# Rings of blocks for scores and probabilities, and an output bank in quarters

## The chip, the core and the metric

The kernel runs on one core of a Trainium2 chip. The metric is the device time of one execution in microseconds, as the median of several runs. A core has five engines that run side by side and are ordered by semaphores: TensorE (PE) for matmuls, VectorE (DVE), ScalarE (ACT), GpSimd (POOL), and SyncE (SP), which issues DMA transfers here.

## The reference, cut to what matters

One layer of an encoder for 2048 prompt rows and 64 sample rows of width 1024. A modulated norm is followed by one input projection; its columns feed four heads of differential attention (two softmaxes, subtracted) and eight heads of forgetting attention (a softmax with a cumulative bias); each result is gated and all go through one output projection.

```python
gate, qa, ka, va, za, qb, kb, vb, zb, logf = project(xp, c_prompt, pos_p, *lw)

def diff_attention(q, k, v, mask, lam):
    s = jnp.einsum('bqhjd,bkhjd->bhjqk', q, k).astype(F32) * (A_QK_DIM ** -0.5)
    p = jax.nn.softmax(jnp.where(mask, s, -jnp.inf), axis=-1)
    a = p[:, :, 0] - lam * p[:, :, 1]
    return jnp.einsum('bhqk,bkhe->bqhe', a.astype(v.dtype), v)

def forgetting_attention(q, k, v, mask, bias):
    s = jnp.einsum('bqhd,bkhd->bhqk', q, k).astype(F32) * (B_DIM ** -0.5) + bias
    p = jax.nn.softmax(jnp.where(mask, s, -jnp.inf), axis=-1)
    return jnp.einsum('bhqk,bkhd->bqhd', p.astype(v.dtype), v)

def merge(x, gate, oa, za, ob, zb, subln_g, lam_init, w_out):
    b, t = x.shape[:2]
    oa = rms_norm(oa, subln_g) * (1.0 - lam_init)
    ga = oa.reshape(b, t, A_WIDTH) * jax.nn.silu(za)
    gb = ob.reshape(b, t, B_WIDTH) * jax.nn.silu(zb)
    o = jnp.concatenate([ga, gb], axis=-1) @ w_out
    return x + gate[:, None, :] * o
```

## The kernel before

The work is cut into eight units. Units 0 to 3 are one differential head each, units 4 to 7 two forgetting heads each; they run in the order 0, 1, 4, 5, 6, 7, 2, 3, the first two interleaved, and the output projection follows. A unit walks over eight blocks of 256 query rows and one block of the sample. A block is projected (matmuls into q with weights wc and activations hT), its queries and keys are normed on ACT, DVE and POOL (u, rs), transposed on PE (tr) and split into a high and a low half in 16 bits.

A row of attention is 128 queries, i from 0 to 15, with i+1 key blocks of 128. Each row has two streams s, which are the two softmaxes of a differential head or the two heads of a forgetting unit. A row goes through these steps:

- PE writes scores into S (`qk_pair`), DVE moves them out into E with mask, bias and maximum (`qk_chunk`).
- ACT takes the exponent in place and sums it (`row_exp`). In a forgetting unit ACT then makes the high half of the probabilities in PB (`row_hi_B`) and DVE the low half (`row_lo_B`).
- SP transposes PB into PT by DMA (`row_trans`), in pieces of eight blocks.
- PE multiplies PT with the values into the bank po (`pv`): per block a matmul of 128 columns and one of 64 in a forgetting unit.
- `outB` reads the forgetting row out of po into og: ACT copies the 64-column halves that hold a lower part, scaled by a number of the unit, DVE adds the upper ones, and two more DVE instructions multiply by the reciprocal of the sum (st) and by the gate g. `outA_sq` and `outA` do it for a differential row. og goes to DRAM (ogd), whence the output projection takes it.

E has three buffers of 16 blocks, PB two of 16, PT seven of eight. A forgetting row of fewer than eight blocks puts both streams into one buffer, a longer one takes a buffer for each. The output bank po is one bank of 512 columns, given out in halves of 256 (`O_tile`); a row takes one half.

The order is made by a planner (class `Plan`). Every step is recorded as an event with a position (`ev`), in the order of positions. The planner gives each instruction a priority from its position, from a table `SHIFT` (one number for each kind of step, engine and slot of the order) and from the buffers that it would have to free, and then lists the instructions of all engines against its own costs; they are issued in the listed order. Each engine runs its instructions strictly in that order. All instructions are issued from one line of the planner, so that the profile gives them all line L547, and tiles tell them apart.

## Time and profile before

| | before |
|---|---|
| median of 3 runs | 1586.65 us (1586.03 to 1587.31) |
| the profiled execution | 1581.7 us |
| its span | 1579.9 us |
| PE busy | 1424.7 us, 90% |
| DVE busy | 1262.2 us, 80% |
| ACT busy | 932.5 us, 59% |
| POOL busy | 508.0 us, 32% |
| DMA queue 1, share of 16 engines | 85.2% |

An engine's busy time tells how much of the span its instructions fill. An engine that waits is told by the views of waits and by the idle time in the groups of instructions, each with the event that ended the wait: "PE po <- DMA PT<-PB" is PE idle before a matmul into po until the transfer from PB to PT had landed. The rows that matter stand in their own section below.

### The profile page before, as it was taken

The numbers are of one execution on the slowest core, as the hardware profiler recorded it, in microseconds if no ns is written. First come the engines' busy times: TensorE is split into PE (matmuls) and PEld (weight loads), VectorE is DVE, ScalarE is ACT, GpSimd is POOL, SyncE is SP. The second block draws the span as 40 slices with busy tenths as digits, with TensorE's granted clock in tenths as the row PEclk, the third lists the DMA queues.
The fourth block names the chain that finished last, engine by engine and source line by source line (L and its number), as shares of the span: only waits on it lengthen the run. The fifth ranks groups of instructions, "written<-read, shape, count | busy, mean of one in ns | idle before, by whom it ended". The sixth has DMA issues, their size and how long they took to land. (4 is left out here: it accounts for less than half of the span.)

```text
span 1579.9 us, 29641 instructions
## 1 busy us (share of the span) xinstructions
PE 1424.7 (90%) x10901; PEld 726.5 (46%) x10901; DVE 1262.2 (80%) x2624; ACT 932.5 (59%) x1772; POOL 508.0 (32%) x620
## 2 busy tenths in 40 slices
PE   6799989889999998988999899988898999699998
PEld 3344445444454444444444454444444444345443
DVE  3989999889778887987798779887798789796531
ACT  2557776666567666765686667656665576453100
POOL 0268564334221112211121112113445354422322
PEclk8899999989999999999999999999999999899999
DMA  9759799659887999999999999899758656698962
GB/s 321 202 149 236 168 205 236 141 114 209 177 186 165 197 236 178 227 196 200 181 255 200 193 205 240 189 204 201 175 138 161 141 139 148 127 199 202 250 178 62
DMA packets 623133, 297.38 MB, mean 188 GB/s; under 512 B 508718, under 2 KB 596414, under 8 KB 615563
## 3 DMA queue, kind: packets, MB, share of 16 engines
q1 hardware_dynamic: 622988, 295.50, 85.2%
q8 instruction: 85, 1.39, 0.4%
q14 instruction: 60, 0.49, 0.1%
HBM read 129.05 MB, written 43.16 MB: 109 GB/s over the span
## 5 line engine op out<-in xcount | busy, mean ns | idle before, releaser
L547 PE MATMUL q<-wc,hT 128*128 128x512 f16 x3072 | 740.4, 385 | 12.3 <-DVE wc L547 2.3
L547 PEld LDWEIGHTS <-hT 128*128 128x128 f16 x3328 | 295.1, 99 | 325.2 <-issue 39.8
L547 ACT ACTIVATE E<-E,st 128x512 f32<-128x512 f32 (+15 forms) x256 | 305.9, 1196 | 155.1 <-DVE st L547 82.9
L547 PE MATMUL po<-VT,PT 128*128 128x128 f16 x3808 | 241.8, 214 | 71.8 <-DMA PT<-PB 44.3
L547 PEld LDWEIGHTS <-PT 128*128 128x128 f16 x3808 | 209.7, 99 | 144.8 <-DMA PT<-PB 61.4
L547 PE MATMUL S<-KT,qT 64*128 64x512 f16 (+3 forms) x1920 | 223.8, 352 | 24.2 <-DVE E L547 13.8
L547 DVE SCALAR_TENSOR_TENSOR PB<-E,PB 128x128 f16<-128x128 f32 (+15 forms) x128 | 165.5, 1302 | 42.4 <-ACT PB L547 42.0
L547 POOL TENSOR_SCALAR rs<-rs 128x8 f32<-128x8 f32 (+1 forms) x72 | 22.4, 311 | 525.4 <-DVE rs L547 518.0
L547 PE MATMUL y<-wc,ogT 128*128 128x512 f16 (+1 forms) x800 | 175.9, 380 | 1.1 <-DVE yt L547 0.9
L547 ACT ACTIVATE PB<-E 128x128 f16<-128x128 f32 (+15 forms) x128 | 139.2, 1103 | 47.4 <-DMA PT<-PB 46.6
L547 DVE CUSTOM_DVE_ANT_0 E<-S,nk,cf 128x1024 f32<-128x1024 f32 (+7 forms) x128 | 131.2, 1044 | 27.8 <-PE S L547 27.2
L547 PEld LDWEIGHTS <-qT 64*128 64x128 f16 x1920 | 85.5, 95 | 147.2 <-issue 83.2
L547 DVE TENSOR_SCALAR_CACHE_REDUCE E<-S,cf 128x1024 f32<-128x1024 f32 (+7 forms) x128 | 130.6, 1044 | 10.1 <-PE S L547 9.5
L547 POOL TENSOR_TENSOR u<-u,gain 128x512 f32<-128x512 f32 (+1 forms) x72 | 100.1, 1391 | 116.5 <-DVE u L547 20.2
L547 POOL TENSOR_TENSOR rs<-rs,mhalf 128x8 f32<-128x8 f32 (+1 forms) x72 | 120.7, 1676 | 5.6
L547 PEld LDWEIGHTS <-ogT 128*128 128x128 f16 (+1 forms) x800 | 76.2, 98 | 93.8 <-issue 7.4
L547 ACT ACTIVATE PB<-E,st 128x128 f16<-128x128 f32 (+7 forms) x64 | 76.7, 1199 | 56.5 <-DVE E L547 20.0
L547 ACT ACTIVATE u<-q,us 128x384 f32<-128x384 f32 x128 | 73.1, 571 | 54.9 <-PE q L547 29.4
L547 DVE SCALAR_TENSOR_TENSOR PB<-E,st,PB 128x128 f16<-128x128 f32 (+7 forms) x64 | 88.5, 1382 | 9.9 <-ACT PB L547 9.5
L547 POOL TENSOR_TENSOR yt<-yt,xr 128x512 f32<-128x512 f32 (+1 forms) x34 | 51.4, 1514 | 120.3 <-DVE yt L547 84.6
L547 POOL TENSOR_SCALAR oar<-oar 128x1 f32<-128x1 f32 (+1 forms) x68 | 31.8, 467 | 152.5 <-ACT og L547 149.4
L547 ACT ACTIVATE og<-po,us 128x128 f32<-128x128 f32 x128 | 45.9, 360 | 50.6 <-PE po L547 46.2
(222 smaller groups left out, 1764.2 us busy)
## 6 DMA issues: line engine op xcount, KB each, us to landing
hT<-hTd SPq DMA_DIRECT2D x53, 1024.0 KB, 5.8
out_dram<-u SPq DMA_DIRECT2D x128, 128.0 KB, 3.1
wc<-in_w_in_dram SPq DMA_DIRECT2D x32, 256.0 KB, 6.6
x<-in_x_prompt_dram SPq DMA_DIRECT2D x16, 512.0 KB, 4.7
hTd<-hT SPq DMA_DIRECT2D x16, 512.0 KB, 3.1
ogd<-og SPq DMA_DIRECT2D x64, 128.0 KB, 2.9
nk<-nck_d SPq DMA_DIRECT2D x16, 512.0 KB, 6.7
xr<-in_x_prompt_dram SPq DMA_DIRECT2D x16, 512.0 KB, 4.6
```

Of the source, the lines that this page charges most:

```text
L547: fn(*a, **kw)
```

## The change

- E, PB and PT become rings of 48, 32 and 56 blocks with the bytes of before (`ring_take`). A row's stream takes i+1 blocks; where they don't fit before the end, the ring starts again at its first block. The weights of the modulation, the first x, its split and the scratch of the first statistics take their space from the rings or from other buffers, and the weights are all loaded in halves.
- The bank po is given out in quarters of 128 columns. A forgetting row takes one for each stream, and `outB` runs for each stream: ACT copies 128x64 scaled by the stream's own reciprocal, DVE adds 128x64 in the same scale. `row_recip` therefore also multiplies the two reciprocals by the unit's number, on ACT. The gate is one product of 128x128 on POOL (`outB_gate`).
- `ev` takes a second position `at`. Events are recorded in the order of `at`, while the priority still comes from the first position; a row's steps now stand together in the record.
- The table `SHIFT` has other numbers throughout; the planner's other numbers are the same.
- The warming matmuls at the head are 176 of 128 columns, not 88 of 256.

```diff
-        po[0] = 256 - po[0]
-        return po[1][:, po[0]:po[0] + 256]
+        po[0] = (po[0] + 128) % 512
+        return po[1][:, po[0]:po[0] + 128]
...
+    rings = dict(E=[0, 48, st([128, 48 * 128], F32, "Ering")], PB=[0, 32, st([128, 32, 2, 128], F16, "PBring")],
+                 PT=[0, 56, st([128, 112, 128], F16, "PTring")])
+
+    def ring_take(name, n):
+        r = rings[name]
+        if r[0] + n > r[1]:
+            r[0] = 0
+        b, r[0] = r[0], r[0] + n
+        if name == "E":
+            return r[2][:, b * 128:(b + n) * 128]
+        return r[2][:, b:b + n] if name == "PB" else r[2][:, 2 * b:2 * (b + n)]
...
-        for _ in range(2 * n):
-            pe.matmul(mod_ps["w"], ident_b, ident_b.unsqueeze(1).broadcast_to([128, 2, 128]), start=True, stop=True)
+        for _ in range(4 * n):
+            pe.matmul(mod_ps["w"], ident_b, ident_b, start=True, stop=True)
...
-            if s == 0 or i >= 8:
-                E_t[g, i, s] = st([128, 2048], F32, f"E{g}_{i}_{s}", tag="E", bufs=3)
-            else:
-                E_t[g, i, 1] = E_t[g, i, 0][:, 1024:2048]
+            E_t[g, i, s] = ring_take("E", i + 1)
...
-        if s == 0 or i >= 8:
-            PB_t[g, i, s] = st([128, 16, 2, 128], F16, f"PB{g}_{i}_{s}", tag="PB", bufs=2)
-            if i < 8:
-                PB_t[g, i, 1] = PB_t[g, i, 0][:, 8:16]
+        PB_t[g, i, s] = ring_take("PB", i + 1)
...
             dve.reciprocal(out=sm[:, 6:8], in_=sm[:, 4:6])
+            act.activation(out=sm[:, 6:8], in_=sm[:, 6:8], func=AF.Copy, scale=usc[g][:, 5:6])
...
-            PT_t[g, i, s, b0 // 8] = st([128, 16, 128], F16, f"PT{g}_{i}_{s}_{b0}", tag="PT", bufs=7)
+            PT_t[g, i, s, b0 // 8] = ring_take("PT", b1 - b0)
...
-        if part == 0 and s == 0:
-            o_ps[g, i] = O_tile()
-        o = o_ps[g, i]
+        if part == 0:
+            o_ps[g, i, s] = O_tile()
+        o = o_ps[g, i, s]
...
-    def outB(g, i, j, t):
-        if t == 0:
+    def outB(g, i, j, t, s):
+
+        if t == 0 and s == 0:
             og_new(g, j)
-        o = o_ps.pop((g, i))[:, 0:256].rearrange("p (s h d) -> p s h d", s=2, h=2)
+        o, sc = o_ps.pop((g, i, s)), st_t.pop((g, i, s))[:, 6 + s:7 + s]
+        w = og_t[g, j][:, t, 64 * s:64 * s + 64]
+        act.activation(out=w, in_=o[:, 64:128], func=AF.Copy, scale=sc)
+        dve.scalar_tensor_tensor(out=w, in0=o[:, 0:64], scalar=sc, in1=w, op0=ALU.mult, op1=ALU.add)
+
+    def outB_gate(g, j, t):
         w = og_t[g, j][:, t, :]
-        w2 = w.rearrange("p (s d) -> p s d", s=2)
-        c = usc[g][:, 5:6]
-        act.activation(out=w2, in_=o[:, :, 1, :], func=AF.Copy, scale=c)
-        dve.scalar_tensor_tensor(out=w2, in0=o[:, :, 0, :], scalar=c, in1=w2, op0=ALU.mult, op1=ALU.add)
-        for s in range(2):
-            d = slice(64 * s, 64 * s + 64)
-            dve.scalar_tensor_tensor(out=w[:, d], in0=w[:, d], scalar=st_t.pop((g, i, s))[:, 6 + s:7 + s], in1=g1_t[g, j][:, t, d],
-                                     op0=ALU.mult, op1=ALU.mult)
+        pool.tensor_tensor(out=w, in0=w, in1=g1_t[g, j][:, t, :], op=ALU.mult)
         if t == 1:
             out_done(g, j)
...
-    def ev(pos, fn, *a):
-        events.append((pos, len(events), fn, a))
+    def ev(pos, fn, *a, at=None):
+
+        events.append((pos if at is None else at, len(events), fn, a, pos))
...
-                    ev(a0 + wd * 0.80, row_exp, g, i, s)
+                    b0 = a + t * 0.5 + 0.40 + 0.01 * s
+                    ev(a0 + wd * 0.80, row_exp, g, i, s, at=b0)
...
-                        ev(a + 1.52 + 0.5 * t, outB, g, i, j, t)
+                                ev(a + 1.00 + 0.5 * t + 0.25 * s + 0.23 * p / npc, pv, g, i, s, p, npc, at=b0 + 0.01 * s)
+                            ev(a + 1.27 + 0.25 * s + 0.5 * t, outB, g, i, j, t, s, at=b0 + 0.005 + 0.01 * s)
+                        ev(a + 1.54 + 0.5 * t, outB_gate, g, j, t, at=b0 + 0.02)
```

On DVE, in unit 5, where rows 11 and 12 follow each other (E_12 and S_12 belong to row 12, the last digit of S_12_0_1 is the chunk of eight blocks; ISA is the evacuation of scores), before:

```order
L547 ISA E_12_0_1246,st_12_0_1247<-S_12_0_0_1244,nk_0_0_1032,cf_196 128x1024 [waits PE_49]
L547 ISA st_12_0_1247 128x1
L547 SCALAR_TENSOR_TENSOR PB_11_0_1239<-E_11_0_1227,PB_11_0_1239 128x12x128 [waits DMAHW1_49,DMAHW0_49,Activation_49]
L547 SCALAR_TENSOR_TENSOR PB_11_1_1240<-E_11_1_1234,PB_11_1_1240 128x12x128 [waits DMAHW3_49,DMAHW2_49,Activation_49]
L547 SCALAR_TENSOR_TENSOR u_8_1241<-q_8_0_1226,us_850,lowr_1242 64x128 [waits Activation_49]
L547 TENSOR_TENSOR qT_7_1249<-tr_7_1248,qT_7_1249 128x256 [waits PE_49,Activation_49]
L547 SCALAR_TENSOR_TENSOR KT_1_1155<-tr_7_1248,sg_192,KT_1_1155 128x256
L547 SCALAR_TENSOR_TENSOR u_8_1241<-q_8_0_1226,us_850,lowr_1242 64x384
L547 ISA E_12_1_1252,st_12_0_1247<-S_12_1_0_1245,nk_1_0_1033,cf_196 128x1024 [waits DVE_49]
L547 ISA st_12_0_1247 128x1
```

and now, where the two low halves of row 11 are the rows that write PBring:

```order
L548 ISA Ering,st_12_0_947<-S_12_0_0_945,nk_0_0_806,cf_195 128x1024 [waits DVE_49,PE_49]
L548 ISA st_12_0_947 128x1
L548 ISA Ering,st_12_0_947<-S_12_1_0_946,nk_1_0_807,cf_195 128x1024 [waits DVE_49,PE_49]
L548 ISA st_12_0_947 128x1
L548 RECIPROCAL st_11_0_937<-st_11_0_937 128x2 [waits Activation_49]
L548 SCALAR_TENSOR_TENSOR og_4_913<-po,st_9_0_917,og_4_913 128x64 [waits Activation_49]
L548 SCALAR_TENSOR_TENSOR g_5_7_923<-g_5_7_923,q_7_1_926 128x128
L548 TENSOR_REDUCE rs_7_939<-sq_7_938 128x8 [waits Activation_49]
L548 SCALAR_TENSOR_TENSOR VT_1_885<-u_7_922,us_696,VT_1_885 128x2x64 [waits Activation_49] x2
L548 ISA Ering,st_12_0_947<-S_12_0_1_950,nk_0_1_877,st_12_0_947,cf_195 128x640 [waits DVE_49,PE_49]
L548 ISA st_12_0_947 128x1
L548 SCALAR_TENSOR_TENSOR PBring<-Ering,PBring 128x12x128 [waits DMAHW6_49,DMAHW7_49,DMAHW5_49,Activation_49]
```

Both streams' first chunks of row 12 stood on either side of the low halves of row 11; they now stand ahead of them, and so does the second chunk of one stream.

On DVE, in the same unit, where row 10 is read out of the bank po into og_5, before (rows that belong to other steps stand between):

```order
L547 SCALAR_TENSOR_TENSOR og_5_1265<-po,us_850,og_5_1265 128x128
L547 TENSOR_REDUCE rs_8_1267<-sq_8_1266 64x4 [waits Activation_49]
L547 SCALAR_TENSOR_TENSOR og_5_1265<-og_5_1265,st_10_0_1211,g_5_5_1148 128x64 [waits DVE_49]
L547 SCALAR_TENSOR_TENSOR og_5_1265<-og_5_1265,st_10_0_1211,g_5_5_1148 128x64
L547 SCALAR_TENSOR_TENSOR g_5_s<-g_5_s,u_8_1241 64x128
```

and now:

```order
L548 ISA Ering,st_12_0_947<-S_12_1_1_951,nk_1_1_878,st_12_0_947,cf_195 128x640 [waits DVE_49,PE_49]
L548 ISA st_12_0_947 128x1
L548 SCALAR_TENSOR_TENSOR og_5_933<-po,st_10_0_927,og_5_933 128x64 [waits Activation_49]
L548 SCALAR_TENSOR_TENSOR og_5_933<-po,st_10_0_927,og_5_933 128x64
L548 SCALAR_TENSOR_TENSOR PBring<-Ering,PBring 128x12x128 [waits DMAHW0_49]
```

Three instructions for the row, one of them over both streams, became two of 64 columns, one for each stream; the product with the gate g stands on POOL.

On PE, in unit 6, where the product of row 14 passes from its first stream to the second, before (PT_14_1_0 is the second stream's first piece):

```order
L547 MATMUL q_2_1_1609<-wc_128,hT_2_1560 128x512
L547 LDWEIGHTS PT_14_1_0_1578 [waits DMAHW3_49]
L547 MATMUL po<-VT_0_1306,PT_14_1_0_1578 128x128
L547 LDWEIGHTS PT_14_1_0_1578
L547 MATMUL po<-VT_0_1306,PT_14_1_0_1578 128x64
```

and now:

```order
L548 MATMUL tr_1_1180<-ident,u_1_1155 128x128 [waits DVE_49,Pool_49]
L548 MATMUL tr_1_1180<-ident,u_1_1155 128x128 x3
L548 LDWEIGHTS PTring [waits DMAHW0_49]
L548 MATMUL po<-VT_0_982,PTring 128x128 [waits Activation_49]
L548 LDWEIGHTS PTring
L548 MATMUL po<-VT_0_982,PTring 128x64
L548 LDWEIGHTS PTring
L548 MATMUL po<-VT_0_982,PTring 128x128 [waits DVE_49]
```

The second stream began behind a projection and waited only for its transpose; it now begins behind the transposes of tr_1 and has a wait for ACT and, two matmuls on, one for DVE, which read po.

## Rows read from the trace of the kernel before

**Rows 1.** Busy us (share of the span) and instructions of each engine, the page.
```profile
PE 1424.7 (90%) x10901; PEld 726.5 (46%) x10901; DVE 1262.2 (80%) x2624; ACT 932.5 (59%) x1772; POOL 508.0 (32%) x620
```

**Rows 2.** PE waits: us in total, times, longest us.
```profile
PE po L547 <- DMA PT<-PB: 44.3, 35, 4.4
PE tr L547 <- POOL u L547: 17.3, 13, 2.6
PE po L547 <- DVE og L547: 17.3, 18, 2.2
PE S L547 <- DVE E L547: 13.8, 11, 8.9
PE po L547 <- ACT og L547: 8.5, 13, 2.3
```

**Rows 3.** Waits of the other engines, the same columns.
```profile
POOL rs L547 <- DVE rs L547: 518.0, 57, 21.9
...
ACT PB L547 <- DMA PT<-PB: 54.4, 30, 6.5
...
DVE wm L547 <- DMA wrow<-wmx_d: 10.7, 4, 5.7
```

**Rows 4.** PE waits for PT in 550:620, 660:780, 840:940 and 1025:1120 us.
```profile
PE po L547 <- DMA PT<-PB: 3.6, 5, 1.5
...
PE po L547 <- DMA PT<-PB: 9.8, 8, 2.1
...
PE po L547 <- DMA PT<-PB: 7.8, 5, 3.8
...
PE po L547 <- DMA PT<-PB: 15.2, 9, 4.4
```

**Rows 5.** Timeline: start us, us, engine, line, operation, [idle before].
```profile
1050.56 0.77 PE L547 MATMUL po<-VT,PT 128*128 128x128 f16 x14 [3.38 <-DMA PT<-PB]
...
1097.69 2.27 DVE L547 SCALAR_TENSOR_TENSOR PB<-E,PB 128x2048 f16<-128x2048 f32 x1
...
1100.00 10.59 SPq L547 DMA_TRANSPOSE PT<-PB  x2
...
1110.97 1.46 PE L547 MATMUL po<-VT,PT 128*128 128x128 f16 x16 [4.39 <-DMA PT<-PB]
```

**Rows 6.** Costliest groups, the page: busy us, mean ns, idle before.
```profile
L547 PE MATMUL q<-wc,hT 128*128 128x512 f16 x3072 | 740.4, 385 | 12.3 <-DVE wc L547 2.3
...
L547 PE MATMUL po<-VT,PT 128*128 128x128 f16 x3808 | 241.8, 214 | 71.8 <-DMA PT<-PB 44.3
```

**Rows 7.** Windows: us, busy of five engines, PEclk, DMA share, GB/s.
```profile
719.00:725.00 6.00, 4.18 (x34) 2.40 (x34) 2.76 (x4) 3.27 (x6) 0.00 (x0) 0.72 1.15 220
1109.00:1115.00 6.00, 4.03 (x37) 2.69 (x38) 0.86 (x3) 1.21 (x3) 0.00 (x0) 0.72 1.05 209
```

**Rows 8.** Groups of lines: busy us, mean ns of one, idle before.
```profile
L547 ACT ACTIVATE og<-po,us 128x128 f32<-128x128 f32 x128 | 45.9, 360 | 50.6 <-PE po L547 46.2 <-issue 2.1 <-DVE og L547 2.1
...
L547 DVE SCALAR_TENSOR_TENSOR og<-og,st,g 128x64 f32<-128x64 f32 x128 | 31.6, 284 | 0.1
...
L547 POOL TENSOR_TENSOR g<-g,sgw 128x256 f32<-128x256 f32 x32 | 26.0, 814 | 40.1 <-DVE g L547 36.1 <-DVE wm L547 1.9 <-DVE wos_e L547 1.8
...
L547 DVE SCALAR_TENSOR_TENSOR og<-po,us,og 128x128 f32<-128x128 f32 x64 | 21.7, 343 | 7.6 <-ACT og L547 4.6 <-PE po L547 2.7
L547 POOL TENSOR_TENSOR u<-rt 128x128 f32<-128x128 f32 (+1 forms) x36 | 21.2, 588 | 2.4
...
L547 ACT ACTIVATE st<-st,lamc 128x1 f32<-128x1 f32 x64 | 18.3, 289 | 16.4 <-DVE st L547 15.2 <-DVE os_e L547 1.0
```

**Rows 9.** Windows, columns as in rows 7.
```profile
440.00:620.00 180.00, 166.16 (x1362) 87.03 (x1360) 142.14 (x311) 117.54 (x224) 35.37 (x35) 0.97 0.95 193
620.00:780.00 160.00, 144.57 (x1218) 74.92 (x1217) 130.02 (x284) 106.77 (x190) 27.47 (x25) 0.97 1.04 206
...
940.00:1120.00 180.00, 161.20 (x1355) 84.66 (x1353) 142.23 (x311) 115.11 (x212) 38.38 (x44) 0.98 1.00 200
```

More of the change, by code (lines that the diff above doesn't have):

```diff
@@ new lines @@
+        'ep_trans PE': (-19798, 2295, 13679, -18706, -16894, -19883, -9078, -20481, 0),
+        'ep_v ACT': (187006, 186641, 186350, 186350, 186350, 187763, 186350, 186350, 0),
+        'ep_v DVE': (94644, 86358, -32098, 180464, 190539, -29803, -13672, 148999, 0),
+        'f_evac ACT': (0, 14022, 0, 0, 0, 0, 0, 0, 0),
+        'f_evac DVE': (0, -10080, 0, 0, 0, 0, 0, 0, 0),
+        'first h ACT': (-26256, 0, 0, 0, 0, 0, 0, 0, 0),
+        'first h DVE': (11632, 0, 0, 0, 0, 0, 0, 0, 0),
+        'first w ACT': (-2265, 0, 0, 0, 0, 0, 0, 0, 0),
@@ new lines @@
+        'first w DVE': (-54089, 0, 0, 0, 0, 0, 0, 0, 0),
+        'first w PE': (-7513, 0, 0, 0, 0, 0, 0, 0, 0),
+        'first w POOL': (-59583, 0, 0, 0, 0, 0, 0, 0, 0),
+        'first x ACT': (-19844, 0, 0, 0, 0, 0, 0, 0, 0),
+        'first x PE': (27289, 0, 0, 0, 0, 0, 0, 0, 0),
+        'first x POOL': (-10481, 0, 0, 0, 0, 0, 0, 0, 0),
[9 rows of a table added]
+        'gate_out ACT': (0, 0, -13137, 0, 0, 0, 0, 0, 0),
+        'gate_out SP d': (0, 0, -30536, 0, 0, 0, 0, 0, 0),
+        'gate_scale DVE': (0, 0, 0, 0, 0, 0, 0, -3073, 30314),
@@ new lines @@
+        'h_load SP d': (4578, 26108, 34022, 38103, 26709, -19849, 31700, 28426, 0),
+        'h_make DVE': (185, 28641, 0, 0, 0, 0, 0, 0, 0),
+        'h_split ACT': (56605, 3935, 0, 0, 0, 0, 0, 0, 0),
+        'h_split DVE': (-3912, 29492, 0, 0, 0, 0, 0, 0, 0),
+        'h_stat ACT': (84300, 21461, 0, 0, 0, 0, 0, 0, 0),
+        'h_stat POOL': (26753, 33714, 0, 0, 0, 0, 0, 0, 0),
+        'h_trans SP d': (4307, 32710, 0, 0, 0, 0, 0, 0, 0),
+        'inp PE': (-909, -3477, -6167, 11921, 1484, 4682, 13216, 4576, 0),
@@ new lines @@
+        'row_hi_B ACT': (0, 0, 25090, 10594, 35533, 4471, -16928, 0, 0),
+        'row_lo_A DVE': (1714, -5614, 64231, 0, 0, 0, 41054, 52495, 55877),
+        'row_lo_B DVE': (0, 0, 27447, 34549, 20418, 7291, 1472, 0, 0),
+        'row_recip ACT': (-14134, 1233, -492, 460, -9256, 1717, -99042, -20606, -77517),
+        'row_recip DVE': (22545, 19098, 23170, 22492, 203432, 9462, 78752, 2250, -74504),
+        'row_trans SP d': (-4346, 23350, 7433, -5677, -5517, 18158, 49608, 2682, 1379),
+        'second x ACT': (-9336, 0, 0, 0, 0, 0, 0, 0, 0),
@@ new lines @@
+        'second x POOL': (-16983, 0, 0, 0, 0, 0, 0, 0, 0),
+        'second x SP d': (1472, 0, 0, 0, 0, 0, 0, 0, 0),
+        'small ACT': (102439, 0, 0, 0, 0, 0, 0, 0, 0),
+        'small DVE': (-290, 0, 0, 0, 0, 0, 0, 0, 0),
+        'small POOL': (432, 0, 0, 0, 0, 0, 0, 0, 0),
+        'small SP d': (125342, 0, 0, 0, 0, 0, 0, 0, 0),
+        'smp_P ACT': (0, -215046, -176136, -182204, -207054, -160922, -203589, -207852, -254163),
+        'smp_P PE': (0, -23517, 6595, -36892, -16617, -32272, -2780, -27414, -10566),
@@ L185 @@
+        'z_post_s ACT': (0, -73115, 44489, -103782, -34487, -82141, 74443, -75360, 0),
+        'z_post_s DVE': (0, 42040, 43541, 41238, 34312, 44523, 42391, 42391, 0),
+        'z_post_s POOL': (0, -83585, 0, 0, 0, 0, 10763, 78, 0),
     }
@@ L1876, in hybrid_layer_kernel @@
     events.sort(key=lambda e: (e[0], e[1]))
-    for pos, _, fn, a in events:
+    for _, _, fn, a, pos in events:
         plan.event(pos, name=fn.__name__)
```

259 lines of the change are left out of this document (105 added, 154 removed), and 30 rows, old and new, of the table SHIFT.

## The prediction

> **What bounds the kernel now.** I read the page's busy times first. TensorE (PE) is busy for 90% of the span, VectorE (DVE) for 80%, ScalarE (ACT) for 59% [rows 1]. So the end is set by PE, and a change can gain only where PE stands still or runs at a low clock. The second view is PE's own waits [rows 2]. The largest is that of the product of probabilities and values (po<-VT,PT) for the transposed probabilities (PT<-PB): 44.3 us in 35 waits. Next come the waits of the same matmuls for the evacuation of the output bank (og read by DVE and by ACT): 17.3 and 8.5 us, 25.8 together. The wait of the scores for E (13.8 us) is mostly one piece of 8.9 us late in the program; DVE waits up to 5.7 us there for the maximum of w_out that goes through DRAM [rows 3].
>
> The third view is where the transposed probabilities come late. I asked for PE's waits over the last six rows (10 to 15) of each of the four forgetting units: 3.6 us in unit 4, 9.8 in unit 5, 7.8 in unit 6, 15.2 in unit 7, 36.4 in all [rows 4]. The timeline shows how such a wait comes about [rows 5]. The last row of unit 7 has its low half made by DVE from 1097.69 for 2.27 us; SyncE issues its two transposes at 1100.00, and they keep the queue until 1110.6; the matmul that needs them starts at 1110.97 after 4.39 us of standing still. Row 12 of the same unit waits 3.38 us before its matmuls of 1050.56. So a row's wait is the length of the chain score, exponent, high and low half, transpose, less the other work that PE has in its order meanwhile.
>
> **The change part by part.**
>
> *Rings.* E, PB and PT keep their bytes; only the grain becomes a block. A row of i+1 blocks needs 2(i+1) of the 32 blocks of PB for its two streams. For i of 11 and more three streams don't fit, so the late rows, those that wait, get no more room in PB than from the two buffers before. ACT's 54.4 us of waiting for PB to be read by the transposes [rows 3] therefore goes mainly in rows that PE does not wait for. Price of the rings by themselves: 0.
>
> *The order.* What can move PE's 36.4 us is the new table of shifts and the rows recorded in a new place. I counted, in both orders, the PE work between a row's last score matmul and its first product matmul, a projection matmul at 740.4/3072 = 0.241 us and a product matmul at 241.8/3808 = 0.0635 us [rows 6]. For row 12 this cover goes from 14.8 to 22.8 us in unit 5, from 17.1 to 21.4 in unit 6, from 14.3 to 21.4 in unit 7, and stays at 15.7 in unit 4. Row 13 loses: 17.6 to 14.8 in unit 6, 16.3 to 14.8 in unit 7. The other late rows change by between -4 and +5 us, most upwards. A wait can shrink by no more than the cover gained. Row by row this takes about 8 us of 9.8 in unit 5, 2 in unit 6, 4 in unit 7 and 1 in unit 4, and gives back 2 in the two rows 13: **-13 us**. The bounds are 0 (the transposes come as late as the cover allows, see the third rival) and -36 (all go). I take the middle because the cover is known to the microsecond and the chain is not: the second streams, which hold the longest wait of 4.39 us, have the same cover as before.
>
> *The clock.* [...] If three go, that is **-5 us**, bounded by 0 and -10.
>
> *The output bank in quarters.* A row of a forgetting unit was evacuated once for both streams, and is now evacuated for each. The orders show what PE pays: the product matmuls that wait for ACT or DVE rise from 132 to 184, and nearly all of them wait for a read of other columns of the same bank, so that the quarter that PE wants is free but its bank is not. By the mean of the waits of before, 25.8/132 = 0.195 us, 52 more cost **+10 us**. From below it is bounded by -26 (all evacuation waits go, since a stream's quarter is free sooner). From above I counted the waits that stand within four PE instructions of the matmul that frees the evacuation, so that nothing covers it: 16 before, 40 now; if these carry the whole 25.8 us, they will carry 64.5, +39. I take the mean price, since only some evacuations are awaited in the trace at all (31 waits make up the 25.8 us, of 132).
>
> *DVE.* It loses 64 instructions of 343 ns and 128 of 284 ns (53.3 us busy) and gains 128 of 64 columns out of PSUM. At the 284 ns of the old 64-column form these make 36.4 us, at 343 ns 43.9: it gains 9 to 17 us [rows 8]. That lies beside PE's work. It is not counted, as a row's chain loses no more than 0.27 us by it.
>
> *ACT.* 64 copies of 360 ns become 128 of half the columns, and 64 scalings of the reciprocals come new. The scaling of one column takes 289 ns [rows 8]; between 289 and 360 ns for a copy the sum is +14 to +23, and with 64 x 0.289 = 18.5 it is **+32 to +42 us of ACT**, half a microsecond a row. ACT has 41% of the span idle, and the exponent and the high half of the next row are queued behind these. If no idle time covered it, 0.6 us for each of the 30-odd rows that wait would be +18; I count 0, because the scaling waits only for a reciprocal that stands just ahead, and hold the +18 within the range.
>
> *GpSimd.* 64 products of 128x128 are new. The nearest rows are 588 and 814 ns [rows 8], so +38 to +52 us. GpSimd waits 518.0 us for DVE's rs alone [rows 3], so that they fit; queued behind each is the next unit's rs, u and gain, which PE's transposes need some slots later. The output rows (ogd) leave SyncE later by the gate, for a reader at the end of the program. Counted 0, up to +4 if some u is held.
>
> *The rest.* The head has the same bytes of weights in five more transfers, and twice as many warming matmuls of half the width: 0, within 2 either way. The 8.9 us of standing still before w_out are kept: DVE waits for the same maximum, with eleven instructions ahead of it in place of twelve.
>
> *Sum.* -13 - 5 + 10 = **-8 us**.
>
> **The rivals.**
>
> *The bank becomes the bound (slower).* Each stream's read of the bank by ACT, then by DVE, holds PE's next stream back although its quarter is free, at the tight price instead of the mean. Then +39 replaces +10 and the sum is +21: 1608 us. It decides from 18 us of new evacuation waits, 0.35 us for each of the 52. For it: 24 new waits have no cover, and two engines read one after the other. Against it: a read takes 0.34 to 0.36 us, and most waits of before are not seen in the trace. Chance 0.30. The Trainium skill, page "PSUM — Partial Sum Buffer", section "PSUM bank collisions raise a hardware error", asks that PSUM be guarded by bank and partition quadrant, not by address; that agrees with the waits on other columns. By that rule waits go with the number of reads of the bank, 256 before and 384 now, +12.9 us, and the sum would be -5.
>
> *The cover suffices everywhere.* With order and ring the late rows' waits all go: -36, the dips behind them -10, evacuation +10: -36, 1551 us. For it: row 12 gains 4 to 8 us where it waited 2 to 4. Against it: rows 13 lose and the second streams gain no cover. Chance 0.15.
>
> *The transposes are bound by the DMA queue.* The mean busy share of the DMA engines is 0.95, 1.04 and 1.00 in three long stretches of the forgetting units [rows 9]. The same bytes move afterwards. If PT comes when the queue lets it, more cover on PE only moves the wait: 0 for waits and dips, and with evacuation between 0 and +10 the time is 1587 to 1597. For it: the transposes of [rows 5] took over 10 us. Against it: early rows under the same share do not wait. Chance 0.15.
>
> **How the numbers follow.** The profiled execution took 1581.7 us, with a span of 1579.9, where the median of the runs is 1586.65, 4.95 above. The sum is made against the profiled one (1573.7) and carried onto the median: 1586.65 - 8 = 1578.65, say **1579 us**, chance 0.40. About 0.2%, 3.2 us, is what a measurement of this kernel tells from no change. Of the forecast's own 0.40 I put 0.05 within it, of the third rival 0.10 within and 0.05 slower; the first rival is slower, the second faster: faster 0.50, same 0.15, slower 0.35. Both signs hold much of the chance, so the forecast's own range is 1568 to 1584. The range of 8 in 10 reaches to the second rival's 1551 and the first's 1608: 1550 to 1608.
>
> **What would show it.** PE's wait for PT should stand at about 31 us instead of 44.3, with row 12 of units 5 to 7 not waiting; its waits for og at about 36 instead of 25.8; DVE's busy time 9 to 17 lower, ACT's 32 to 42 and GpSimd's 38 to 52 higher; PE's matmul time unchanged. The forecast is wrong if the og waits pass 44 us, if PT's stay above 40, if PE waits for GpSimd's u more than the 17.3 us of before [rows 2], or if a new gap opens at the head or at w_out.

## The result: 1598.68 us after, 0.64% slower than before

| | before | after |
|---|---|---|
| median of 5 runs | 1586.65 us (1586.03 to 1588.39) | 1598.68 us (1592.78 to 1599.70) |
| the profiled execution | 1581.7 us | 1594.2 us |
| its span | 1579.9 us | 1592.4 us |

The ratio over all runs of the pair is 1.0064, with a 95% interval of 1.0047 to 1.0081; the two medians of the table alone would give 1.0076. The forecast was 1579 us, so the sign was wrong; the time lies within the range. The two profiled executions differ by 12.5 us of span, and what follows says where these lie.

The page's busy line of the kernel after [rows 1] and its PE waits [rows 2] (us in total, times, longest us):

```profile
PE 1432.1 (90%) x10989; PEld 735.1 (46%) x10989; DVE 1245.3 (78%) x2560; ACT 955.0 (60%) x1900; POOL 536.1 (34%) x684
```

```profile
PE po L548 <- DMA PTring<-PBring: 47.3, 25, 8.9
PE po L548 <- ACT og L548: 24.4, 31, 3.2
PE po L548 <- DVE og L548: 19.2, 24, 2.9
PE tr L548 <- POOL u L548: 15.9, 12, 4.4
...
PE S L548 <- DVE Ering L548: 4.4, 4, 3.1
```

The waits for og are 43.6 us in place of 25.8. The wait for the transposes looks the same, 47.3 beside 44.3, but it holds another thing: its longest piece, 8.9 us, stands at w_out, where before the scores waited 8.9 us for E. DVE waits there for the maximum of w_out, as in before (6.3 us beside 5.7), so the piece says nothing of the transposes. Outside it the waits for them are 38.4 us.

**Where the 12.5 us are.** I laid the two traces side by side at points where PE had done about the same work (the counts of its instructions differ by 5 at most). Unit 1's tail, the four forgetting units and the rest are three windows of each kernel. Of before, then of after (us; busy time and instructions of PE, PEld, DVE, ACT, POOL; PEclk; DMA share; GB/s):

```profile
372.00:434.00 62.00, 59.31 (x463) 30.39 (x460) 51.40 (x96) 37.14 (x72) 21.36 (x27) 1.00 0.93 187
434.00:1162.00 728.00, 662.63 (x5473) 344.73 (x5472) 595.57 (x1304) 488.72 (x916) 157.14 (x167) 0.98 0.98 200
1162.00:1579.90 417.90, 382.73 (x2533) 190.05 (x2531) 295.15 (x560) 180.32 (x332) 159.49 (x192) 0.98 0.68 159
```

```profile
369.00:438.00 69.00, 63.41 (x464) 31.72 (x461) 49.85 (x87) 36.55 (x67) 15.77 (x22) 0.93 0.98 163
438.00:1176.00 738.00, 663.92 (x5476) 349.59 (x5473) 578.91 (x1244) 509.44 (x1043) 199.95 (x235) 0.97 0.98 198
1176.00:1592.40 416.40, 384.16 (x2538) 190.30 (x2535) 297.62 (x567) 182.56 (x339) 151.60 (x188) 0.98 0.65 160
```

Up to unit 1's tail after is 3 us ahead (369 beside 372). The tail loses 7, the forgetting units lose 10, the rest gives back 1.5: -3 + 7 + 10 - 1.5 = 12.5. In the forgetting units PE's busy time grew by 1.3 us only; its idle time went from 728.0 - 662.6 = 65.4 to 74.1 us. By the names of the waits there, the transposes fell from 38.0 to 33.0 us, and the evacuations of the output bank rose from 17.8 to 32.1, before and then after:

```profile
PE po L547 <- DVE og L547: 12.2, 13, 2.2
PE po L547 <- ACT og L547: 5.6, 8, 2.3
...
PE po L548 <- ACT og L548: 18.7, 22, 3.2
PE po L548 <- DVE og L548: 13.4, 16, 2.9
```

Going by the names alone, one would put the whole growth down to the bank; the first experiment shows that this would be wrong.

In the tail 4.1 of the 7 us are busy time of about as many instructions (464 beside 463), and the granted clock is the difference to be seen: 0.93 beside 1.00. Three windows of after there, the same columns:

```profile
381.00:387.00 6.00, 2.94 (x18) 1.25 (x16) 6.00 (x7) 2.17 (x3) 3.22 (x5) 0.74 1.05 99
387.00:393.00 6.00, 6.00 (x45) 3.35 (x45) 4.81 (x10) 4.72 (x7) 0.00 (x0) 0.69 1.07 157
417.00:423.00 6.00, 6.00 (x55) 4.67 (x54) 2.15 (x6) 2.49 (x6) 2.42 (x4) 0.72 0.95 255
```

and the two PE instructions ahead of which it stood still (start, us, operation, [idle before]):

```profile
384.84 2.10 PE L548 MATMUL S<-KT,qT 64*128 64x512 f16 x11 [3.06 <-DVE Ering L548]
...
416.76 3.51 PE L548 MATMUL po<-VT,PTring 128*128 128x128 f16 x42 [2.28 <-DMA PTring<-PBring]
```

Around each of the two waits the granted clock was at 1.2 in place of 2.4 GHz for a part of the stretch (0.74 and 0.69, then 0.72). Before had no such wait there, and its clock in the tail is 1.00. It doesn't fall with every long wait: around the wait of 3.38 us that ended at 1050.56 in before [rows 5] it stayed at 1.00 (columns as above).

```profile
1047.00:1053.00 6.00, 2.62 (x26) 1.31 (x27) 3.94 (x8) 4.54 (x5) 4.57 (x7) 1.00 1.50 226
```

**Where the longer cover went.** I took the PE waits for transposes in the four forgetting units row by row, by the order of the product matmuls (us, units 4, 5, 6, 7, and the sum):

| row | before | after |
|---|---|---|
| 12 | 0.9, 2.3, 5.7, 4.4: 13.3 | 1.4, 2.1, 0, 0: 3.4 |
| 13 | 0.8, 2.1, 0, 1.4: 4.3 | 1.6, 2.2, 0.4, 2.5: 6.7 |
| 14 | 0.4, 0, 0, 3.3: 3.7 | 4.0, 0.4, 6.1, 0: 10.5 |
| 15 | 1.5, 2.0, 1.1, 5.1: 9.7 | 0.9, 4.2, 1.8, 1.0: 7.8 |
| all 16 | 38.0 | 33.0 |

Row 12 won 10 us, and rows 13 and 14 lost 9. The two long waits of row 14 are new, in units 4 and 6:

```profile
596.01 1.30 PE L548 MATMUL po<-VT,PTring 128*128 128x128 f16 x14 [3.98 <-DMA PTring<-PBring]
...
936.94 1.30 PE L548 MATMUL po<-VT,PTring 128*128 128x128 f16 x14 [6.10 <-DMA PTring<-PBring]
```

Ahead of them the four transposes of the row took 16.58 and 16.90 us on SyncE, where the same row of unit 4 took 9.91 in before (after, after, before):

```profile
583.57 16.58 SPq L548 DMA_TRANSPOSE PTring<-PBring  x4
...
924.30 16.90 SPq L548 DMA_TRANSPOSE PTring<-PBring  x4
...
580.55 9.91 SPq L547 DMA_TRANSPOSE PT<-PB  x4
```

Why they took so much longer there isn't shown.

In row 12 of unit 5 the cover had grown most, from 14.8 to 22.8 us, and yet it waits 2.05 us for its transposes (before: 2.07). It is the one row 12 of units 5 to 7 that still waits, and it shows how cover can come to nothing. First ACT and DVE of after (the high and the low halves are the rows that write PBring), then PE:

```profile
704.80 2.86 ACT L548 ACTIVATE PBring<-Ering 128x1536 f16<-128x1536 f32 x2 [0.85 <-DMA PTring<-PBring]
...
707.76 1.67 ACT L548 ACTIVATE Ering<-Ering,st 128x1664 f32<-128x1664 f32 x1
...
717.90 3.07 ACT L548 ACTIVATE PBring<-Ering 128x1664 f16<-128x1664 f32 x2 [1.56 <-DMA PTring<-PBring]
```

```profile
704.34 0.94 DVE L548 CUSTOM_DVE_ANT_0 Ering<-S,nk,st 128x640 f32<-128x640 f32 x1
...
706.32 1.76 DVE L548 SCALAR_TENSOR_TENSOR PBring<-Ering,PBring 128x1536 f16<-128x1536 f32 x1 [1.04 <-ACT PBring L548]
...
710.15 1.75 DVE L548 SCALAR_TENSOR_TENSOR PBring<-Ering,PBring 128x1536 f16<-128x1536 f32 x1
...
719.52 3.69 DVE L548 SCALAR_TENSOR_TENSOR PBring<-Ering,PBring 128x1664 f16<-128x1664 f32 x2 [1.97 <-ACT PBring L548]
```

```profile
727.87 0.77 PE L548 MATMUL po<-VT,PTring 128*128 128x128 f16 x14 [2.05 <-DMA PTring<-PBring]
```

and SyncE:

```profile
708.11 8.67 SPq L548 DMA_TRANSPOSE PTring<-PBring  x4
```

The same row in before, ACT, DVE and PE:

```profile
703.90 1.68 ACT L547 ACTIVATE E<-E,st 128x1664 f32<-128x1664 f32 x1 [3.09 <-DVE st L547]
...
707.37 1.58 ACT L547 ACTIVATE PB<-E 128x1664 f16<-128x1664 f32 x1
...
709.45 1.89 DVE L547 SCALAR_TENSOR_TENSOR PB<-E,PB 128x1664 f16<-128x1664 f32 x1
...
720.58 0.85 PE L547 MATMUL po<-VT,PT 128*128 128x128 f16 x16 [2.07 <-DMA PT<-PB]
```

In after the exponent of row 12 (1664 columns) is done at 707.76 + 1.67 = 709.43. Its high half starts at 717.90, 8.5 us later. Row 11 (1536 columns) is being halved meanwhile, at 706.32 and 710.15, and its transposes keep SyncE until 716.78; but only the last 1.56 us ahead of the high half are a wait for them. The rest of the 8.5 us ACT spends on what its order lists in between: the exponent of the other stream, work on the next block and copies of og, with some 2 us of waiting for DVE. In before the exponent was done at 705.58, the high half came 1.8 us later and the low half at 709.45. So the scores of row 12 did go ahead of the halves of row 11, as the order showed, and PE had more work meanwhile; but what followed the scores came later by about as much. From the end of the last evacuation of scores of the row's first stream (704.34 + 0.94) to the end of its low half it is 16.1 us, where it was 7.5. In units 4 to 7 this piece of row 12's chain went from 7.5, 7.5, 7.7 and 6.3 us to 7.5, 16.1, 12.8 and 14.7: it grew by 0, 8.6, 5.1 and 8.4 where the cover grew by 0, 8.0, 4.3 and 7.1. In units 6 and 7 the wait went all the same, because from the low half to the first product it now took 5.4 and 5.1 us in place of 8.1 and 9.2.

### The profile page after: what moved, and what is told of

The parts are those of the page before. It is cut to its first block, busy times and chain, and to the rows that moved or that the text cites. A ratio compares the mean times of both kernels' runs of the same rounds, so it can differ in the third digit from the quotient of the medians.

```text
span 1592.4 us, 30008 instructions
## 1 busy us (share of the span) xinstructions
PE 1432.1 (90%) x10989; PEld 735.1 (46%) x10989; DVE 1245.3 (78%) x2560; ACT 955.0 (60%) x1900; POOL 536.1 (34%) x684
## 5 line engine op out<-in xcount | busy, mean ns | idle before, releaser
L548 ACT ACTIVATE Ering<-Ering,st 128x512 f32<-128x512 f32 (+15 forms) x256 | 306.0, 1197 | 115.6 <-DVE Ering L548 61.3
L548 PE MATMUL po<-VT,PTring 128*128 128x128 f16 x3808 | 250.6, 217 | 92.9 <-DMA PTring<-PBring 47.3
L548 PEld LDWEIGHTS <-PTring 128*128 128x128 f16 x3808 | 216.7, 101 | 162.9 <-issue 72.4
L548 DVE SCALAR_TENSOR_TENSOR PBring<-Ering,PBring 128x512 f16<-128x512 f32 (+15 forms) x128 | 166.5, 1316 | 43.2 <-ACT PBring L548 41.8
L548 ACT ACTIVATE PBring<-Ering 128x128 f16<-128x128 f32 (+15 forms) x128 | 138.8, 1104 | 30.8 <-DMA PTring<-PBring 24.7
L548 DVE CUSTOM_DVE_ANT_0 Ering<-S,nk,cf 128x1024 f32<-128x1024 f32 (+7 forms) x128 | 130.1, 1045 | 25.5 <-PE S L548 25.2
L548 POOL TENSOR_TENSOR og<-og,g 128x128 f32<-128x128 f32 x64 | 46.2, 723 | 299.0 <-DVE og L548 275.4
L548 DVE TENSOR_SCALAR_CACHE_REDUCE Ering<-S,cf 128x1024 f32<-128x1024 f32 (+7 forms) x128 | 130.3, 1043 | 11.0 <-PE S L548 10.8
L548 ACT ACTIVATE PBring<-Ering,st 128x384 f16<-128x384 f32 (+8 forms) x64 | 76.4, 1200 | 62.8 <-DVE Ering L548 31.2
L548 DVE SCALAR_TENSOR_TENSOR PBring<-Ering,st,PBring 128x384 f16<-128x384 f32 (+9 forms) x64 | 87.2, 1366 | 5.3 <-ACT PBring L548 5.0
L548 DVE SCALAR_TENSOR_TENSOR Ering<-Ering,st 128x640 f32<-128x640 f32 (+9 forms) x64 | 88.8, 1392 | 0.5
```

What stands on the lines that cost most here:

```text
L548: fn(*a, **kw)
```

## The experiments

All ratios are to the kernel before on the same chip. The kernel after was not run again beside them, so that its 1.0064 comes from another chip than most of what it is set beside; differences of 0.1 to 0.3% between ratios say little. Where an experiment keeps an order, it is the kernel's own listed order, written out by number, so that the edit moves nothing else.

**Is it the bank?** The reads of po by the evacuations are taken from a constant tile at issue, in after and in before.

```diff
-        act.activation(out=w, in_=o[:, 64:128], func=AF.Copy, scale=sc)
+        act.activation(out=w, in_=other(ident[:, 64:128], o[:, 64:128]), func=AF.Copy, scale=sc)
```

> The changed kernel in its own order, with every read of the output bank po by ScalarE and VectorE (copies, squares, sums, gates of all rows) taken from a constant SBUF tile of the same shape in place of po, so that no matmul waits for an evacuation and no evacuation for a matmul; the attention results are left out of the output by that. Bank theory (the second stream's own evacuation holds TensorE at the bank): TensorE's 43.6 us of waiting for og go and no other wait takes their place; 1598.7 - 36 to 48 = 1551 to 1563 us. Transposes theory (the changed order makes PT late, and whatever is won before a row is waited for at PT): the waits for PT grow from 47 to 70 us or more, and the time falls by less than 20, to above 1579.

> The kernel before in its own order, with the same reads of po taken from a constant tile. Bank theory: its 25.8 us of waiting for og go, 1586.65 - 20 to 28 = 1559 to 1567 us, and the distance of 12 us between the two kernels is gone (within 4 either way) or turned round. Transposes theory: the distance between this run and the changed kernel without reads stays 8 us or more.

After without reads: 1604.2 us, 1.0050 (1.0029 to 1.0070). Before without reads: 0.9944 (0.9925 to 0.9964). PE's waits of after without reads:

```profile
PE po L736 <- DMA PTring<-PBring: 67.7, 29, 10.3
PE tr L736 <- POOL u L736: 20.8, 17, 4.4
PE S L736 <- DVE st L736: 14.6, 19, 2.0
```

No wait for og is left, and 20 of its 43.6 us came up again as waits for transposes, 13 as waits of scores for DVE. What is gained is less than in before, and the distance between the two kernels is 1.1%, not smaller. So the waits for the bank, with the evacuations' reads, are not what separates them.

A second look at the same question gave the rows back their single time of evacuation: in 61 of the 64 rows both streams are read out where the second one was, and 139 product matmuls wait in place of 184.

```diff
+                    last.calls, o.calls = o.calls + last.calls, []
```

> The changed kernel in its own order, where in 61 of the 64 forgetting rows the first stream's two evacuating instructions are issued where the second stream's are, so that each row is read out once, at its end; the product matmuls with a wait on ScalarE or VectorE fall from 184 to 139. Bank theory: the waits for og fall from 43.6 to about 26 us, the time to 1598.7 - 18 = 1581 us (1576 to 1588). Transposes theory: 1595 to 1600 us, og's waits turning into waits for PT.

1605.97 us, 1.0060 (1.0036 to 1.0083): no change to after's 1.0064. The waits for og fell to 34.9 and those for PT rose to 66.7.

**Which part of the change?** Each part is taken out of after alone, and the new table is put into before; the planner lists anew in these four. The new recording order (`at`) was not tried by itself and stays in the first three.

> The changed kernel with the fixed buffers of before for E, PB and PT (and the weights and x where they lay before); quarters, gate on GpSimd, recording order and new table stay, and the planner lists it anew. Theory that the rings are the cause (a row's first stream lies over blocks of the row before's second stream, so that its high half waits for that stream's transposes): the ratio to the kernel before goes from 1.0064 to 1.000 or below. Theory that the table and the recording order are the cause: the ratio stays above 1.004; without the room that the table was made for it may go past 1.01.

> The changed kernel with the output bank in halves and a forgetting row read out at once, its gate on VectorE and no scaling of the reciprocals on ScalarE, as before; rings, recording order and new table stay, and the planner lists it anew. Theory that quarters with their extra work on ScalarE (+22 us busy) and GpSimd are the cause, not by the bank but by ScalarE's queue: the ratio goes from 1.0064 to 1.000 or below. Rings or table the cause: it stays at 1.004 to 1.010.

> The changed kernel with the table of shifts of the kernel before; rings, quarters and recording order stay, and the planner lists it anew. Theory that the new table's order makes the forgetting units slow: the ratio goes to 1.002 or below. Structure (rings, quarters) the cause: it stays at 1.006 or goes above, up to 1.03, since the old table was not made for it.

> The kernel before (fixed buffers, halves) with the table of shifts of the changed kernel, listed anew by the planner. With the changed kernel under the old table at 1.017 this closes the square: if the table is worse by itself, 1.01 to 1.02 here; if structure and table only fit each other, also above 1.005; if the new table is better by itself and the structure costs the 0.64%, 0.995 or below.

The edits, in this order:

```diff
-        PB_t[g, i, s] = ring_take("PB", i + 1)
+            PB_t[g, i, s] = st([128, 16, 2, 128], F16, f"PB{g}_{i}_{s}", tag="PB", bufs=2)
...
-        po[0] = (po[0] + 128) % 512
+        po[0] = 256 - po[0]
...
-    SHIFT = {...}
+    SHIFT = {...}
```

| | ratio to before |
|---|---|
| after, buffers in place of rings (E and PT likewise) | 1.0525 (1.0495 to 1.0555) |
| after, halves in place of quarters, one `outB` a row, warming matmuls of 256 columns | 1.0176 (1.0146 to 1.0207) |
| after with the table of before | 1.0170 (1.0139 to 1.0201) |
| before with the table of after | 1.0224 (1.0196 to 1.0252) |
| after | 1.0064 (1.0047 to 1.0081) |

With its own table each structure is better than with the other's: old and old 1.0000, old and new 1.0224, new and old 1.0170, new and new 1.0064. A part of each misfit may be that the tables differ in their steps: the old one has no number for `outB_gate`, the new one none for the old `outB`. Beside the new table the rings and the quarters gain 4.6% and 1.1%; what they would do beside a table made for them alone wasn't tried, so the price of a part can't be told apart from the order that it is listed in. The run with the table of after in before shows where such a misfit goes (PE waits): mostly to transposes and scores.

```profile
PE po L548 <- DMA PT<-PB: 63.6, 40, 6.2
PE S L548 <- DVE E L548: 24.6, 20, 6.0
```

**Is it the loads ahead of the transposes, or the room in PB?** SyncE's queue holds loads of nk and hT ahead of the transposes that are late. Eight nk loads were moved behind them in after; then 26 loads of hT in after and 21 in before.

```diff
+            self.order.remove(o)
+            self.order.insert(self.order.index(near[3]) + 1, o)
```

> The changed kernel in its own order, save that eight 512 KB loads of nk that SyncE issues just ahead of the transposes of late rows are issued behind them. Bank theory: 1595 to 1600 us. Transposes theory, in the form that these loads hold the transposes that take 10 to 12 us: the three waits for PT of 4.0, 4.2 and 6.1 us go and with them dips of the clock, 1598.7 - 14 to 18 = 1581 to 1585 us, unless the first rows of the next unit now wait for nk (VectorE E waiting for nk, up to 5 us in four units).

> The changed kernel in its own order, save that 26 loads of hT (1 MB each, for the next block's projection) that SyncE issues just ahead of transposes in the forgetting units are issued behind the first one or two of these. Theory that the loads ahead hold the late rows' transposes and that these set the pace: the transposes of 10 to 12 us that rows 14 and 15 wait for fall to 5, TensorE's waits for PT from 47 to 30 us or less, the ratio from 1.0064 to 0.995 to 1.001. Theory that the transfers' sum sets the pace whatever their sequence: PT's waits fall, waits of the projection for hT take their place, ratio 1.004 to 1.012.

> The kernel before in its own order, with 21 such loads of hT issued behind the first one or two transposes. Sequence theory: PT's waits from 44 to 30 us or less, ratio 0.990 to 0.996. Sum theory: 0.998 to 1.006.

After with nk later: 1.0142 (1.0087 to 1.0198); with hT later: 1.0242 (1.0217 to 1.0267), PT waits 75.8 us; before with hT later: 1.0065 (1.0039 to 1.0090), PT waits 51.7. Each is slower than before, and the two of after are slower than after. PE's waits for transposes gained nothing by it: with nk later they stay at 47.3 us in all, and the two long waits of row 14 stand in both runs of after (5.0 and 6.0 us, 4.7 and 5.9).

For the room, rows of eleven and more blocks got either half of PB for each stream, as the old buffers gave it, in after's order:

```diff
+        if name == "PB" and n > 10:
+            r[0] = (r[0] + 15) // 16 * 16 % r[1]
+            b, r[0] = r[0], r[0] + 16
```

> The changed kernel in its own order, in which rows of 11 and more blocks take their PB at block 0 or block 16 of the ring, in turn, so that a stream waits for the stream two before it alone and never for two streams. Rings the cause by that coupling: ScalarE's waits of PB for transposes (29.4 us) fall by half, the ratio goes from 1.0064 to 1.001 or below. Otherwise 1.004 to 1.008.

1.0139 (1.0103 to 1.0175), PT waits 59.7 us. In this order the old grain of PB is worse; so the new grain is not shown to be the loss.

**Is it the transfers?** The 144 stores of new keys and values, 17.3 of 297.4 MB, were left out in both kernels; then they were kept and issued from GpSimd.

```diff
+            if o.kind in ("ep_kout SP d", "ep_square SP d"):
+                continue
...
+                if o.kind in ("ep_kout SP d", "ep_square SP d"):
+                    fn = self.pool._r.dma_start
```

> The kernel before in its own order, without the 144 stores of new keys and values (128 of them 128 KB, issued by SyncE); those outputs are left out. Between 434 and 1115 us SyncE is occupied for 578 of 681 us, 448 of it in transposes and 38 in these stores. Queue theory (SyncE with its transfers, not TensorE, sets the pace of the forgetting units): the stores' own time there, 38 us, comes off in large part, the whole run gets 15 to 45 us shorter (ratio 0.97 to 0.99), and the waits for PT fall from 44 to below 30. Order theory (the chain over VectorE and ScalarE sets it, the queue has room): ratio 0.997 to 1.000.

> The changed kernel in its own order, without the same 144 stores; those outputs are left out. SyncE is occupied for 576 of 694 us in the forgetting units here, 42 in these stores. Queue theory: 15 to 45 us shorter than the changed kernel (ratio to the kernel before 0.975 to 0.995). Order theory: ratio 1.003 to 1.006.

> The changed kernel in its own order, with the 144 stores of new keys and values issued from GpSimd, where most of their data is made, at the same places of the order; the same bytes move. If SyncE's issuing is what is short, the ratio falls from 1.0064 to 0.99 or so, as without the stores. If the transfers themselves are short, nothing is won: 1.003 to 1.008. If GpSimd is held up by waiting for its stores, it is slower, up to 1.02.

> The kernel before in its own order, with the same stores issued from GpSimd. SyncE's issuing short: ratio 0.985 to 0.995, a version faster than both. Transfers short: 0.997 to 1.003. GpSimd held up: up to 1.015.

Without the stores: before 0.9879 (0.9852 to 0.9906), after 0.9910 (0.9879 to 0.9941). Issued from GpSimd: before 1.0021 (0.9995 to 1.0047), after 1.0086 (1.0053 to 1.0119). So leaving out the bytes gains 1.2% in before and some 1.5% in after, and issuing them from GpSimd gains nothing. Without the stores the two kernels lie 0.3% apart (1.0031, interval 1.0009 to 1.0053), and the waits of row 14 in units 4 and 6 fall to 3.4 and 1.0 us. That distance is smaller than with the stores, but the two intervals still overlap a little, and the PT waits of both kernels only fell to 41.1 us, where less than 30 had been expected. A part of the loss may hang on the transfers; these runs don't settle it. The forgetting units of the two runs without stores, before and then after, in the columns of the windows above:

```profile
436.00:1149.90 713.90, 660.61 (x5472) 345.33 (x5471) 595.51 (x1303) 488.02 (x913) 157.70 (x166) 0.97 0.95 190
```

```profile
436.60:1158.70 722.10, 663.63 (x5470) 349.14 (x5468) 578.51 (x1246) 509.06 (x1042) 199.94 (x235) 0.97 0.93 188
```

They are some 14 and 16 us shorter than the windows of the kernels with the stores, traced on another chip, with 7% fewer bytes in them (713.9 us x 190 GB/s beside 728 x 200). Length doesn't follow bytes one to one here. PE is idle for 53.3 and 58.5 us in place of 65.4 and 74.1, so the transfers have a part in its idle time, and not all of it goes with them.

**Does PE wait for the transposes at all?** In both kernels the product matmuls take a tile of the values as weights in place of the transposed probabilities, which are still made and moved; a third run takes the reads of the bank away as well.

```diff
+            w = VT[g, kb // 8][:, kb % 8].rearrange("p a d -> p (a d)")[:, 0:128]
+            plan.alt[id(hi)] = plan.alt[id(lo)] = w
```

> Kernel before in its own order, but every product matmul takes a tile of the values as its weights in place of the transposed probabilities (a part of the computation is changed; the transposes are still issued and moved, and nothing reads them). PE can't wait for a transpose any more. Theory 1, the chain score, exponent, halves, transpose, product sets the pace as PE sees it: the 44 us of waits for PT go and nothing takes their place, 25 to 50 us, ratio to before 0.968 to 0.984. Theory 2, the pace is that of the transfers and of SyncE's queue: the waits come up again as waits for hT, nk or the buffers of scores, ratio 0.994 to 1.0. Theory 3, the loss of the changed kernel lies in the order of the other work and has nothing to do with transposes: like theory 1 here, but see the next run.

> Changed kernel, same edit (a part of the computation is changed). Theory 1: the 47 us of waits for PT go and the gap of 0.64% to the kernel before closes: it stands within 0.25% of the run before. Theory 2: ratio to before 1.0 to 1.006, the gap stays. Theory 3: it gains as much as the run before does and the gap stays at 0.4 to 1.0%.

> Changed kernel with neither wait: product matmuls take the values as weights, and the evacuations read a constant tile in place of the bank (two parts of the computation are changed). If evacuation waits are covered by the wait for transposes (theory 1), they show their own price once those are gone: 15 to 40 us below the run with the first edit alone. If the pace is that of the transfers (theory 2), nothing more: within 5 us of it.

Before: 0.9923 (0.9899 to 0.9948). After: 1.0020 (1.0000 to 1.0039). After with neither: 0.9997 (0.9976 to 1.0018). The 44.3 us of PT waits were worth 12 us of time in before; in after it is some 7 us for the 47.3, if the two chips may be compared. The distance between the kernels stayed, at 1.0%. Waits of the run of before, of PE, ACT and DVE:

```profile
PE S L732 <- DVE E L732: 22.1, 13, 8.5
...
PE S L732 <- DVE st L732: 17.3, 16, 3.1
```

```profile
ACT PB L732 <- DMA PT<-PB: 68.4, 40, 7.8
```

```profile
DVE PB L732 <- ACT PB L732: 62.4, 53, 7.9
```

The scores now wait for DVE's evacuation (17.3 us in place of 4.8 for st); DVE waits for ACT's high half (62.4 beside 51.5), and ACT waits for room in PB, that is for the same transposes (68.4 beside 54.4 [rows 3]). In after the last of these goes from 29.4 to 49.5. The waits have moved to the other end of the transpose. Of the forgetting units, windows of the three runs in the order told:

```profile
435.00:1158.30 723.30, 663.57 (x5471) 349.32 (x5470) 595.02 (x1303) 487.43 (x914) 154.08 (x167) 0.97 0.99 201
```

```profile
435.50:1173.70 738.20, 667.67 (x5469) 351.24 (x5468) 580.74 (x1246) 508.83 (x1043) 200.58 (x235) 0.97 0.97 197
```

```profile
437.50:1166.40 728.90, 664.69 (x5469) 349.14 (x5468) 583.83 (x1244) 509.85 (x1042) 200.13 (x235) 0.97 0.98 200
```

PE is idle for 59.7, 70.5 and 64.2 us there, beside 65.4 and 74.1 with all waits in place. My reading, which no run tests by itself, is that PE is a follower in these units: the ring of scores, exponent, halves, transposes and room in PB goes round at its own pace. DVE is busy for 82% and less of it, so no single engine is full; the DMA engines' mean share is 0.97 to 0.99 in all three. With the transposes out of PE's way, taking the reads of the bank away as well gave 0.9997 in place of 1.0020; the intervals overlap, so a price of the evacuation waits isn't shown by it.

**What is settled and what is open.** Settled: 7 of the 12.5 us lie in unit 1's tail and 10 in the forgetting units, with 4.5 given back elsewhere; the distance between the kernels doesn't go when PE's waits for the bank, or those for the transposes, are taken away from both. With neither, after is as fast as the whole of before (0.9997), but before with neither was not run. Moving loads or giving PB its old room made after slower. Each structure is faster with its own table than with the other's. Open: why PE's two waits in unit 1's tail came about, which rows of the new table cost the 10 us, why the transposes of row 14 became slow, and how much of the distance hangs on the transfers, as it shrank to 0.3% without the stores. No run isolates a single row, and no run that computes everything was faster than before.

## Why the prediction was wrong, step by step

**The order, -13 us: the step that failed.** PE's waits for PT in the forgetting units were to fall by 13 us, and went from 38.1 (4.9, 10.2, 7.8, 15.2) to 33.0 us (7.0, 11.4, 8.3, 6.3), so -5. The count of PE's work was right for row 12, and its waits fell by 10. But the step took everything else as fixed ("the cover is known to the microsecond and the chain is not"), and counted no loss for row 14. The same edit that gave the cover put the row's scores ahead of the previous row's halves, so that the piece of the chain behind them grew by as much in units 5 to 7; in unit 5, where 8 of 9.8 us were to go, the waits grew to 11.4, and row 12, which was to wait no more, waits 2.05. Row 14, whose cover did not shrink, waits 6.8 us more, behind transposes of 16.58 and 16.90 us; row 13 gives back 2.4, close to the 2 that were counted. In unit 7 the waits shrank by 9 where 4 had been counted. The second failure is under the first: even a shorter wait isn't a shorter time. All PT waits together, 44.3 us, were worth 12 us in before, so that the full price of a microsecond of PT wait, by which the sum went, was nearly four times too high (44.3 / 12). Why the transposes of row 14 came late, and which rows of the table cost the 10 us of the forgetting units, stays open.

**The clock, -5 us.** The wrong sign. No run shows a gain of 5 us by the clock. There were six dips to 1.2 GHz around PT waits in the forgetting units of before, and I find five in after; PE's busy time there is the same (+1.3). Dips don't go with waits one by one: around the 3.38 us wait that ended at 1050.56 in before the clock stayed at 1.00. In unit 1's tail two new ones came, around waits of 3.06 us for DVE and 2.28 us for a transpose, with +4 us of busy time. PE's matmul time, which was to stay the same, is 7.4 us longer in all (1424.7 to 1432.1).

**The evacuation, +10 us.** As waits +17.8 us: 0.34 us for each of 52, just under the 18 from which the first rival was to decide, and under its 39. The Trainium skill, page "PSUM — Partial Sum Buffer", section "PSUM bank collisions raise a hardware error", asks for a guard by bank and not by address; the trace agrees, as the waits stand ahead of matmuls into other columns of the bank that is read. That the waits go with the number of reads was the prediction's own step; it gave +12.9, and the trace shows 17.8. As time they cost little in this order: the first experiment took them all away, and the time hardly moved.

**DVE, ACT, GpSimd.** DVE -16.9 us (9 to 17 forecast), but that sum had set busy time of the old rows (53.3) against means times counts of the new, so the fit is partly luck. The ACT rows that the change touches cost +32 us as forecast: the copies 37.3 us for 128 and the scalings 17.9 for 64, in place of half of 45.9. The page shows only +22.5 in all, below the 32 to 42 forecast; why ACT's other rows took less wasn't followed. The product on POOL is 46.2 us, 723 ns each, within 588 and 814; the page shows +28.1 in all, below the 38 to 52. No run gives any of these as a term of the time, and PE waits for u 15.9 us beside 17.3. The groups are:

```profile
L548 POOL TENSOR_TENSOR og<-og,g 128x128 f32<-128x128 f32 x64 | 46.2, 723 | 299.0 <-DVE og L548 275.4 <-DVE st L548 16.8 <-issue 6.5
L548 ACT ACTIVATE og<-po,st 128x64 f32<-128x64 f32 x128 | 37.3, 308 | 27.6 <-PE po L548 26.0 <-DMA wc<-in_w_in_dram 0.6 <-DVE og L548 0.3
...
L548 ACT ACTIVATE st<-st,us 128x2 f32<-128x2 f32 x64 | 17.9, 290 | 9.3 <-DVE st L548 9.2
```

**Rings, head, w_out at 0.** The 8.9 us at w_out stayed, as said, under another name. The head is 3 us ahead. The rings at 0 can't be judged alone: beside the new table, taking them out costs 4.6%.

**The rivals.** The first had the right sign by the wrong road: its waits came at half its price, and taking them away leaves the distance between the kernels. That 1598.68 lies within the range of 1550 to 1608 is owed to this rival's bound, and is luck for the forecast's own mechanism. The second is wrong: the waits of row 12 mostly went, but those of rows 13 to 15 rose from 17.7 to 25.0 us. The third came nearest. It said that more cover only moves the wait where transfers set the pace, 0 for waits and dips; that leaving out bytes shortened both kernels, and that freeing PE from the transposes moved the wait to PB's other end, is in keeping with it but doesn't show that the queue set the pace. Its 1587 to 1597 stops short of the 1598.68, and it had no term for an order that makes a part of the chain longer or for the tail's lower clock.

## What to carry to other kernels

In this kernel 44.3 us of waits of the busiest engine were worth 12. Before such a wait is priced, follow it to the other end of the buffer (who waits for the same transfer to free its source?), and price it by that loop. When a reordering gives one engine more cover, follow the same steps on the other engines, and count every row and not only those that wait now: here work moved ahead of a chain's earlier link came with a chain that was longer by about as much, and a row that had hardly waited gave back much of what another won. And where a planner's table is tuned to a structure, structure and table are one change: taken apart, each of the four pairs says something else.

## What was not expected

Taking tens of microseconds of PE's waits away leaves most of its idle time in the forgetting units: 59.7 to 74.1 us in five kernels, of which three had no wait for transposes and one of these none for the bank. And some 7% fewer bytes in a stretch with a DMA share of 0.98 shortened it by 2%, while the share fell to 0.95 and 0.93: a share near 1 did not make the length go with the bytes here.
